# The odd layer's input projection: halves of rotated blocks taken one block later, and all its stores moved to the load queue

## The chip, the cores and the metric

The kernel runs on one core of one Trainium2 chip. The metric is the device time of one execution in microseconds (us). TensorE is called PE, VectorE DVE, ScalarE ACT, GpSimd POOL and SyncE SP. SP does nothing but issue DMAs. Line numbers (L1675) are those of the kernel before; in the changed kernel the same statements stand 2 to 14 lines further down.

## The reference, cut to what matters

A two-layer network on 256 context tokens and 2048 latent tokens of width 1024. Layer 0 (Fourier mixing and latent attention) is left as it is. Layer 1, the odd one, is grouped-query attention in a window of 128 tokens; this is what it projects:

```
q, k, v, g = split_cols(h_lat @ w_in, ODD_SPLITS)      # 1024, 256, 256, 1024 columns
q = apply_rope(q.reshape(b, n, 4, 4, 64), *rope)       # x1*cos - x2*sin, x2*cos + x1*sin
k = apply_rope(k.reshape(b, n, 4, 64), *rope)
ck, cv = split_cols(h_ctx @ w_in[:, 1024:1536], (256, 256))      # context: k and v, not rotated
y_l = (windowed_gqa(q, k, v, ck, cv, sink_hg) * silu(g)) @ w_out
```

## The kernel before, in words

**Items.** The tokens form nine chunks of 256 (chunk 0 is the context). The odd layer's input projection, at about 1820 to 2340 us of the span, walks over 15 steps, n = 0 to 14. A step is a group of chunks (1, 2, 3; then 4, 5, 6, 0; then 7, 8) with one block of 512 columns of the weights: the two halves of q, k with v, the two halves of the gate. In the first two groups the order is q, q, k/v, gate, gate (n = 0 to 4 and 5 to 9); in the third it is gate, gate, q, q, k/v (n = 10 to 14). A step consists of items (chunk i, half j), six for a q step of three chunks; an item of q, k or v is 48 matmuls of 128x256 into one of six PSUM banks (`ppm`). Every factor is held as two rounded halves, high and low, hence three products for one (`mm3`, L186 to L188).

**After an item.** `finish_t` rotates a q or k block: DVE multiplies by the two tables (L1675, L1676; the reading of PSUM ends here), POOL adds and subtracts (L1677, L1678), ACT rounds to the high half `rh` (L1679) and POOL subtracts for the low half `rl` (L1680). `rh` and `rl` have two buffers each. `store_t` writes the halves to DRAM (`q1h`, `q1l`, `kTh`, `kTl`) in four DMAs of 128 KB, issued by ACT (L1665). They are put in the list `pend`, and `flush` issues them behind the arithmetic of the next item. v goes through L1772, L1779, L1780 to `vd` (L1782), the gate through L1785 and L1789 to `g1d` (L1790), with ACT issuing too.

**Loads, all from SP.** While a step runs, the weights of the next (four loads of 512 KB) and later chunks of the input (`h1d`, two loads of 512 KB) come in and are split into halves by ACT (L180) with DVE or POOL (L183). The rope tables (`in_c_rope1c`, `in_c_rope1s`, 128 KB) have two buffers per kind; a step asks for its first two chunks' at its start and for the third's one chunk later. In step 1 eight blocks of weights of 128 KB (`in_o_w_in_t` 128x256, `bnd_load`) pass through two buffers: DVE takes absolute values (L1635) and PE multiplies (L1636), for a bound on v.

**The next stage** begins inside steps 13 and 14. `load_q6` loads the stored q of a query block of 128 tokens and one of four key heads in three DMAs (`sbr<-q1h`, `sbr<-q1l`). PE forms scores for the maxima (L1525, L1538) and DVE reduces them (L1529); then come the scores themselves (L1813 to L1815), ACT's exponentials (L1820) and the products with v (L1831 to L1833).

**What sets the order.** A scheduler puts the instructions of each engine in an order of its own. Only SP's DMAs are kept in the order of the program text: the class `sp` wraps each in `keep_in_program_order` (L150). An engine, SP too, issues in order and stands at an instruction that waits. Besides, each DMA waits until the one eight places before it, of SP's and ACT's together, has landed.

Of the kernel before, what the change touches and what calls it, by code (L numbers as in the profile page):

```python
# [10 lines left out]
F32 = mybir.dt.float32  # L11
F32R = mybir.dt.float32r
# [9 lines left out]
P = 128  # L22
# [119 lines left out]
def tile_hybrid(ctx: ExitStack, tc: tile.TileContext, A, out, dumps=None, stop=99):  # L142
    nc = tc.nc
    dumps = dumps or {}
    pe, act, dve, pool = nc.tensor, nc.scalar, nc.vector, nc.gpsimd
# [460 lines left out]
    for pi, chs in enumerate(PASSES):  # L606
# [12 lines left out]
        for oi, (ct, ci) in enumerate(order):  # L619
            if ct > seen:  # L620
# [4 lines left out]
                if ct >= 2 and nlater < len(later):  # L625
                    j = nlater
# [207 lines left out]
    for n_, (g, k) in enumerate(order):  # L834
# [14 lines left out]
        if k in (1, 3):  # L849
            q = ap_.tile([P, 512], F32, tag="qs", name=f"qs{g}_{k}")  # L850
            act.copy(q, res[k])
            if k == 1:
                pv = res[0][:, :, 0:256]
# [135 lines left out]
    def halves(dst, rows, src, n, name, e_lo=dve):  # L989

        eh = ep2.tile([P, 512], F32, tag="eh", name=f"{name}h")
        el = ep2.tile([P, 512], F32, tag="el", name=f"{name}l")
        act.copy(eh[:, 0:n].bitcast(F32R), src[:, 0:n])
        e_lo.tensor_sub(el[:, 0:n].bitcast(F32R), src[:, 0:n], eh[:, 0:n])
        flush2()

        def go():
            for d, r in zip(dst, (eh, el)):
                if isinstance(rows, int):
                    act.dma_start(d.rearrange("(h f d) t -> f h d t", f=2, d=16)[rows], r[:, 0:n])  # L1000
                else:
                    act.dma_start(d[rows, :], r[:, 0:n])

        pend2.append(go)
# [4 lines left out]
    for ci, (t0, n) in enumerate(CH):  # L1009
# [5 lines left out]
        for j in range(4):  # L1015
# [5 lines left out]
            e = ep2.tile([P, 512], F32, tag="eh", name=f"ek{ci}_{j}")  # L1021
# [581 lines left out]
    c5, b5, ep5 = sbuf(), sbuf(2), sbuf(3)  # L1603
# [51 lines left out]
    pend = []  # L1655

    def flush():
        while pend:
            pend.pop(0)()

    def store_t(rh, rl, i, rows):
        for r, kd, qd in ((rh, kTh, q1h), (rl, kTl, q1l)):
            dst = (kd[i] if rows is None else qd[i - 1][rows, :]).rearrange("(h f d) t -> f h d t", f=2, d=32)
            for f in range(2):
                act.dma_start(dst[f], r[:, f])  # L1665

    def finish_t(ps, n, i, rows):
        pv = ps.rearrange("p (f t) -> p f t", f=2)
        rh = ep5.tile([P, 2, 256], F32, tag="rh", name=f"rh5_{n}_{i}", bufs=2)
        rl = ep5.tile([P, 2, 256], F32, tag="rl", name=f"rl5_{n}_{i}", bufs=2)  # L1670
        if i:
            r = ep5.tile([P, 2, 256], F32, tag="ev", name=f"rt5_{n}_{i}")
            ct, st = (tabs[n, i, nm][:, None, :].to_broadcast([P, 2, 256]) for nm in ("ct", "st"))
            t = ep5.tile([P, 2, 256], F32, tag="tr", name=f"tt5_{n}_{i}", bufs=2)
            dve.tensor_mul(r, pv, ct)  # L1675
            dve.tensor_mul(t, pv[:, ::-1, :], st)  # L1676
            pool.tensor_sub(r[:, 0], r[:, 0], t[:, 0])  # L1677
            pool.tensor_add(r[:, 1], r[:, 1], t[:, 1])  # L1678
            act.copy(rh.bitcast(F32R), r)  # L1679
            pool.tensor_sub(rl.bitcast(F32R), r, rh)  # L1680
        else:
            act.copy(rh.bitcast(F32R), pv)
            dve.tensor_sub(rl.bitcast(F32R), pv, rh)
        flush()
        pend.append(lambda: store_t(rh, rl, i, rows))

    for n, (p, b) in enumerate(seq):
        bi = n % 5
        items = [(i, j) for i in P5[p] for j in range(2) if b == 2 or i]
        tb = [i for i in P5[p] if i] if b < 3 else []  # L1690
        for i in tb[0:1]:
            tab_load(n, i)
        fill = []
        if n == 0:
            fill += h5_steps(2) + fill5 + h5_steps(3)
        if n == 1:
            for q in (sm4, ppt):
                q.close()
            ppx = psum(2)
            fill += [bnd_open] + [lambda k=k: bnd_mm(k) for k in range(KT)] + [bnd_fin]  # L1700
        if p < 2:
            if bi == 3:
                fill += h5_steps(P5[p + 1][0])
        if p == 0 and bi == 4:
            pass
        if n == 10:
            x4p.close()
            x4p.tile([P, 2, 512], F32, tag="x", bufs=4)
            hs.close("s0", "s1")
        fill += w5_steps(n + 1)  # L1710
        late = []
        if p < 2 and bi == 4:
            late = P5[p + 1][1 : 3]
        if n == 5:
            fill = h5_steps(0) + fill
        e6n = []
        if n >= 11:
            e6n = e6.pop(0)
        tot = len(items) * KT
        done = 0  # L1720
        nf, ne = len(fill), len(e6n)
        w6n = []
        if n == 14:
            early6 = [f for x in range(TP["wa"] + 1) for f in (([lambda x=x: wload(*wl_[x])] if x < TP["wa"] else []) + ([lambda x=x: wsplit(*wl_[x - 1])] if x else []))]
            w6n, early6 = early6[:4], early6[4:]
        for x, (i, j) in enumerate(items):
            hh, hl = h5t[i]
            js = slice(j * P, (j + 1) * P)
            if b < 3 and not j and i in tb and tb.index(i) + 1 < len(tb):
                tab_load(n, tb[tb.index(i) + 1])  # L1730
            ps = ppm.tile([P, 512], F32, tag="mm", name=f"m5_{n}_{i}_{j}")
            for kk in range(KT):
                if b > 2:
                    wh, wl = w5t[n, kk]
                    mm3(ps, hh[:, kk, js], hl[:, kk, js], wh, wl, kk == 0, kk == KT - 1)
                else:
                    f, k0 = divmod(kk, 4)
                    o = ps[:, f * 256 : (f + 1) * 256]
                    fs = slice((2 * j + f) * P, (2 * j + f + 1) * P)
                    fj = slice(f * P, (f + 1) * P)  # L1740
                    for k in (2 * k0, 2 * k0 + 1):
                        wh, wl = w5t[n, k]
                        if b == 2 and j:
                            mm3(o, hh[:, k, fj], hl[:, k, fj], wh[:, 256:512], wl[:, 256:512], k == 0, k == KT - 1)
                        else:
                            mm3(o, wh[:, fs], wl[:, fs], hh[:, k, :], hl[:, k, :], k == 0, k == KT - 1)
                done += 1
                while fill and nf - len(fill) < nf * done / tot:
                    fill.pop(0)()
                while e6n and ne - len(e6n) < ne * done / tot:  # L1750
                    e6n.pop(0)()
                if w6n and done % 3 == 0:
                    w6n.pop(0)()
            if n == 14 and x == 1:
                while w6n:
                    w6n.pop(0)()
                hs.close("s2")
                w6n = early6
            if j == 1 and late:
                k_ = late.pop(0)  # L1760
                fs = h5_steps(k_)
                nf += len(fs)
                fill = fs + fill
            if b < 2:
                finish_t(ps, n, i, slice(b * 512 + j * 256, b * 512 + j * 256 + 256))
                continue
            if b == 2 and not j:
                finish_t(ps, n, i, None)
                continue
            e = ep5.tile([P, 512], F32, tag="ev", name=f"e5_{n}_{i}_{j}")  # L1770
            if b == 2:
                dve.tensor_mul(  # L1772
                    e.rearrange("p (f c) -> p f c", f=2), ps.rearrange("p (f c) -> p f c", f=2),
                    scl1[:, None, :].to_broadcast([P, 2, 256]),
                )
                vt = ep5.tile([P, 8, VW], F16, tag="vt", name=f"vt5_{n}_{i}", bufs=2)
                ev = e.rearrange("p (h d) -> p h d", d=64)
                pool.memset(vt[:, :, 64:VW], 1.0)
                act.copy(vt[:, :, 0:64], ev)  # L1779
                pool.tensor_sub(vt[:, :, 65:129], ev, vt[:, :, 0:64])  # L1780
                for f in range(2):
                    act.dma_start(vd[2 * i + f], vt[:, 4 * f : 4 * f + 4])  # L1782
            else:
                hf = b - 3
                act.activation(e, ps, AF.Silu)  # L1785
                ev = e.rearrange("p (k h d) -> p k h d", k=2, d=64)
                uv = uns1[:, hf * 128 : hf * 128 + 128].rearrange("p (k d) -> p k d", d=64)[:, :, None, :]
                for kk in range(2):
                    pool.tensor_mul(ev[:, kk], ev[:, kk], uv[:, kk].to_broadcast([P, 4, 64]))  # L1789
                act.dma_start(g1d[2 * i + j - 2][:, hf * 512 : (hf + 1) * 512], e)  # L1790
        flush()
        for f in fill + e6n + w6n:
            f()
        if n == 13:
            wgt.close(*[f"{t}{n % 2}{k}" for t in "hl" for k in range(KT)])
# [349 lines left out]
```

## Time and profile before

| | before |
|---|---|
| median of 3 runs | 3030.02 us (3030.01 to 3030.97) |
| profiled execution | 3034.24 us, span 3032.2 us |
| mean granted clock of PE | 0.983 |
| busy, share of the span | PE 94%, POOL 54%, DVE 48%, ACT 47% |

The span is what the trace covers, and all starting times are counted from its beginning. The granted clock is the share of PE's full speed that the chip allows; 1.00 is 2.4 GHz, 0.50 is 1.2 GHz. A busy time counts neither semaphore waits nor the issue of DMAs.

### The profile page before, as it was taken

To read this page: it belongs to the slowest core of one execution; us is meant where nothing else is said; L and a number is where in the kernel's file an instruction comes from. 1 tells how busy PE (TensorE), PEld (TensorE's weight loads), DVE (VectorE), ACT (ScalarE), POOL (GpSimd) and SP (SyncE) were. 2 spreads that over 40 slices of the span, in tenths; PEclk is the share of its full clock that TensorE was granted. 3 is DMA by queue.
4 is the path that set the end of the run, shared out by engine and by line. 5 is a ranking of instruction groups with operands and counts; after the bars stand their busy time and mean duration, and the time that the engine had idled before them with its cause. 6 is when DMAs were issued, how large, how long until landed. Compare 5 with 4: busy or idle time off the path is not lost. (4 is left out here: it accounts for less than half of the span.)

```text
span 3032.2 us, 54284 instructions
## 1 busy us (share of the span) xinstructions
PE 2861.0 (94%) x21388; PEld 2299.7 (76%) x21388; DVE 1462.6 (48%) x2884; ACT 1427.4 (47%) x2131; POOL 1632.0 (54%) x1221
## 2 busy tenths in 40 slices
PE   7999999999999999999999998999997899999998
PEld 4787777877777777777777888989786666677666
DVE  3323315453656665666542234323234666676664
ACT  4333213223577777777773332232222645554554
POOL 2202204035588888888784434353443766766665
PEclk9999999999999999999999998999998999999999
DMA  6453335466310111011016545544464333223321
GB/s 240 153 177 134 130 122 173 142 213 223 104 44 26 44 40 44 26 44 40 26 35 232 188 153 177 187 141 162 152 189 156 105 105 98 84 77 93 102 83 45
DMA packets 299399, 357.13 MB, mean 118 GB/s; under 512 B 40884, under 2 KB 210172, under 8 KB 299144
## 3 DMA queue, kind: packets, MB, share of 16 engines
q1 hardware_dynamic: 231320, 258.73, 27.0%
q10 hardware_dynamic: 67824, 94.93, 8.9%
q8 instruction: 168, 2.75, 0.4%
q14 instruction: 87, 0.71, 0.1%
HBM read 245.82 MB, written 107.76 MB: 117 GB/s over the span
## 5 line engine op out<-in xcount | busy, mean ns | idle before, releaser
L186 PE MATMUL psb<-sbr 128*128 128x512 f32 (+3 forms) x2054 | 744.3, 363 | 14.4 <-ACT sbf L1022 5.7
L188 PE MATMUL psb<-sbr 128*128 128x512 f32 (+3 forms) x2054 | 722.9, 352 | 4.8 <-DVE sbr L183 4.8
L187 PE MATMUL psb<-sbr 128*128 128x512 f32 (+3 forms) x2054 | 723.8, 352 | 2.2 <-POOL sbr L183 2.2
L1188 POOL TENSOR_TENSOR sbf<-sbf 128x1024 f16<-128x1024 f32 (+1 forms) x296 | 624.2, 2112 | 140.8 <-ACT sbf L1187 76.9
L155 PE MATMUL psb<-sbr 100*128 100x512 f32 (+1 forms) x2408 | 624.2, 399 | 21.0 <-DVE sbr L955 14.4
L155 PEld LDWEIGHTS psb<-sbr 100*128 100x128 f32 (+1 forms) x2408 | 425.0, 190 | 112.8 <-issue 17.3
L942 DVE TENSOR_REDUCE sbf<-psb 128x1 f32<-128x512 f32 (+1 forms) x584 | 400.7, 690 | 218.1 <-PE psb L155 203.5
L186 PEld LDWEIGHTS psb<-sbr 128*128 128x128 f32 (+1 forms) x2054 | 390.7, 190 | 81.0 <-issue 12.3
L188 PEld LDWEIGHTS psb<-sbr 128*128 128x128 f32 (+1 forms) x2054 | 390.2, 190 | 63.9 <-DVE sbr L183 6.8
L187 PEld LDWEIGHTS psb<-sbr 128*128 128x128 f32 (+1 forms) x2054 | 390.8, 190 | 53.2 <-POOL sbr L183 3.9
L1821 POOL TENSOR_TENSOR sbf<-sbf 128x512 f16<-128x512 f32 x282 | 338.0, 1213 | 116.0 <-issue 60.1
L1186 ACT ACTIVATE sbf<-psb 128x1024 f32<-128x1024 f32 (+1 forms) x296 | 299.6, 1012 | 200.4 <-PE psb L155 180.5
L183 DVE TENSOR_TENSOR sbr<-sbf,sbr 128x512 fp32r<-128x512 f32 (+3 forms) x212 | 209.1, 1014 | 382.2 <-ACT sbr L180 381.1
L180 ACT CAST sbr<-sbf 128x512 fp32r<-128x512 f32 (+4 forms) x286 | 198.2, 731 | 394.5 <-PE psb L187 149.5
L183 POOL TENSOR_TENSOR sbr<-sbf,sbr 128x512 fp32r<-128x512 f32 (+4 forms) x113 | 166.1, 1482 | 367.9 <-ACT sbr L180 226.3
L1819 ACT ACTIVATE sbf<-psb 128x512 f32<-128x512 f32 x312 | 188.4, 604 | 282.1 <-PE psb L1815 249.8
L1187 ACT ACTIVATE sbf<-psb 128x1024 f16<-128x1024 f32 (+1 forms) x296 | 297.8, 1006 | 0.0
L155 PEld LDWEIGHTS <-sbf 128*128 128x128 f16 x4672 | 213.5, 97 | 72.9 <-issue 65.9
L155 PE MATMUL psb<-sbf 128*128 128x129 f16 (+1 forms) x4672 | 256.8, 207 | 5.2 <-DVE sbf L1214 2.9
L1529 DVE CUSTOM_DVE_ANT_0 sbf<-psb,sbf 128x384 bf16<-128x384 f32 (+1 forms) x256 | 137.8, 538 | 119.4 <-PE psb L1525 108.1
L1820 ACT ACTIVATE sbf<-psb 128x512 f16<-128x512 f32 x312 | 188.2, 603 | 5.5 <-DMA vd<-sbf 5.5
L1831 PEld LDWEIGHTS <-sbf 128*128 128x128 f16 x1248 | 115.5, 97 | 68.3 <-issue 61.8
(259 smaller groups left out, 4303.9 us busy)
## 6 DMA issues: line engine op xcount, KB each, us to landing
sbf<-in_o_w_in_t SPq DMA_DIRECT2D x60, 512.0 KB
sbf<-in_w_in_t SPq DMA_DIRECT2D x54, 512.0 KB
sbf<-in_x SPq DMA_DIRECT2D x32, 512.0 KB
sbf<-in_w_mod SPq DMA_DIRECT2D x32, 512.0 KB
sbr<-q1h SPq DMA_DIRECT2D x128, 128.0 KB
h1d<-sbf ACTq DMA_DIRECT2D x9, 1024.0 KB
sbf<-h1d SPq DMA_DIRECT2D x18, 512.0 KB
x1d<-sbf ACTq DMA_DIRECT2D x16, 512.0 KB
```

The costliest lines, as they stand in the source:

```text
L155: tc.keep_in_program_order(nc.tensor.matmul(*args, **kw))
L180: act.copy(hi, src)
L183: e_lo.tensor_sub(lo, src, hi)
L186: pe.matmul(ps, sh, mh, start=start, stop=False)
L187: pe.matmul(ps, sh, ml, start=False, stop=False)
L188: pe.matmul(ps, sl, mh, start=False, stop=stop)
L942: dve.reduce_max(st["mx"][:, js[0] : js[-1] + 1, c], ps[:, 0 : len(js) * kn].rearrange("p (j k) -> p j k", k=kn), axis=AX.X)
L1186: act.activation(pf[:, :, 0:n], ps[:, :, 0:n], AF.Exp, scale=MLA_SCALE)
L1187: act.activation(ph[:, :, 0:n], ps[:, :, 0:n], AF.Exp, scale=MLA_SCALE)
L1188: pool.tensor_sub(pl[:, :, 0:n], pf[:, :, 0:n], ph[:, :, 0:n])
L1819: act.activation(pf, ps, AF.Exp, scale=GQA_SCALE)
L1821: (dve if (TP["b0"].get("sub", TP["sub"]) if b == 0 else TP["sub"])[kv][n] else pool).tensor_sub(pl, pf, ph)
```

## The change

`flush` no longer empties the list but runs as many entries as stood in it on entry. A rotated block now enters `pend` with its halving; run at the next item, the halving puts the store in the list, and the item after that issues it. So halves are taken one item later and stored one more. At the end of a step `while pend: flush()` empties the list. The unrotated k of the context is halved at once. The stores of q, k, v and the gate are issued by `sp.dma_start`, so on SP, in the order of the program text among the loads, where ACT issued them; those of v and the gate too wait one item.

```diff
--- before.py
+++ after.py
@@ -1655,19 +1655,21 @@
     pend = []
 
     def flush():
-        while pend:
+        for _ in range(len(pend)):
             pend.pop(0)()
 
     def store_t(rh, rl, i, rows):
         for r, kd, qd in ((rh, kTh, q1h), (rl, kTl, q1l)):
             dst = (kd[i] if rows is None else qd[i - 1][rows, :]).rearrange("(h f d) t -> f h d t", f=2, d=32)
             for f in range(2):
-                act.dma_start(dst[f], r[:, f])
+                sp.dma_start(dst[f], r[:, f])
 
     def finish_t(ps, n, i, rows):
         pv = ps.rearrange("p (f t) -> p f t", f=2)
-        rh = ep5.tile([P, 2, 256], F32, tag="rh", name=f"rh5_{n}_{i}", bufs=2)
-        rl = ep5.tile([P, 2, 256], F32, tag="rl", name=f"rl5_{n}_{i}", bufs=2)
+
+        def halves():
+            return [ep5.tile([P, 2, 256], F32, tag=t, name=f"{t}5_{n}_{i}", bufs=2) for t in ("rh", "rl")]
+
         if i:
             r = ep5.tile([P, 2, 256], F32, tag="ev", name=f"rt5_{n}_{i}")
             ct, st = (tabs[n, i, nm][:, None, :].to_broadcast([P, 2, 256]) for nm in ("ct", "st"))
@@ -1676,13 +1678,22 @@
             dve.tensor_mul(t, pv[:, ::-1, :], st)
             pool.tensor_sub(r[:, 0], r[:, 0], t[:, 0])
             pool.tensor_add(r[:, 1], r[:, 1], t[:, 1])
+        else:
+            flush()
+            rh, rl = halves()
+            act.copy(rh.bitcast(F32R), pv)
+            dve.tensor_sub(rl.bitcast(F32R), pv, rh)
+            pend.append(lambda: store_t(rh, rl, i, rows))
+            return
+        flush()
+
+        def halve():
+            rh, rl = halves()
             act.copy(rh.bitcast(F32R), r)
             pool.tensor_sub(rl.bitcast(F32R), r, rh)
-        else:
-            act.copy(rh.bitcast(F32R), pv)
-            dve.tensor_sub(rl.bitcast(F32R), pv, rh)
-        flush()
-        pend.append(lambda: store_t(rh, rl, i, rows))
+            pend.append(lambda: store_t(rh, rl, i, rows))
+
+        pend.append(halve)
 
     for n, (p, b) in enumerate(seq):
         bi = n % 5
@@ -1778,8 +1789,9 @@
                 pool.memset(vt[:, :, 64:VW], 1.0)
                 act.copy(vt[:, :, 0:64], ev)
                 pool.tensor_sub(vt[:, :, 65:129], ev, vt[:, :, 0:64])
+                flush()
                 for f in range(2):
-                    act.dma_start(vd[2 * i + f], vt[:, 4 * f : 4 * f + 4])
+                    pend.append(lambda d=vd[2 * i + f], v=vt[:, 4 * f : 4 * f + 4]: sp.dma_start(d, v))
             else:
                 hf = b - 3
                 act.activation(e, ps, AF.Silu)
@@ -1787,8 +1799,10 @@
                 uv = uns1[:, hf * 128 : hf * 128 + 128].rearrange("p (k d) -> p k d", d=64)[:, :, None, :]
                 for kk in range(2):
                     pool.tensor_mul(ev[:, kk], ev[:, kk], uv[:, kk].to_broadcast([P, 4, 64]))
-                act.dma_start(g1d[2 * i + j - 2][:, hf * 512 : (hf + 1) * 512], e)
-        flush()
+                flush()
+                pend.append(lambda d=g1d[2 * i + j - 2][:, hf * 512 : (hf + 1) * 512], e=e: sp.dma_start(d, e))
+        while pend:
+            flush()
         for f in fill + e6n + w6n:
             f()
         if n == 13:
```

What this does to the order shows at three places. The first is SP at the end of step 0. Before, with the loads of the next step's weights, the tables of step 1 and the eight blocks of the bound in a row (`h1d3` is the input of chunk 3, `sbf_62` on-chip memory):

```order
L150 DMA sbf_62<-h1d3_5182 128x4x256 x2
L150 DMA sbf_62<-in_o_w_in_t 128x2x512 x4
L150 DMA sbf_62<-in_c_rope1c 128x256
L150 DMA sbf_62<-in_c_rope1s 128x256
L150 DMA sbf_62<-in_c_rope1c 128x256
L150 DMA sbf_62<-in_c_rope1s 128x256
L150 DMA sbf_62<-in_o_w_in_t 128x256 x8
```

Now, from the stores of the third item on (`q1h1` is chunk 2's high half; each row is two DMAs):

```order
L150 DMA sbf_62<-in_o_w_in_t 128x2x512 x2
L150 DMA q1h1_15987<-sbf_62 4x32x256 x2
L150 DMA q1l1_15995<-sbf_62 4x32x256 x2
...
L150 DMA q1h2_15988<-sbf_62 4x32x256 x2
L150 DMA q1l2_15996<-sbf_62 4x32x256 x2
L150 DMA sbf_62<-in_c_rope1c 128x256
L150 DMA sbf_62<-in_c_rope1s 128x256
L150 DMA sbf_62<-in_c_rope1c 128x256
L150 DMA sbf_62<-in_c_rope1s 128x256
L150 DMA sbf_62<-in_o_w_in_t 128x256 x8
```

All stores of step 0 stand ahead of step 1's tables and of the eight blocks. The same holds wherever q or k steps follow one another. The first store of step 1 in turn stands behind the eight blocks. On PE the first product with such a block (L1636) was the 41st matmul of step 1 and is now the 80th; from it to the seventh there were 72 matmuls and are now 66.

The second place is ACT in step 0, at the splits of chunk 3's input (L180). Before:

```order
L1665 DMA q1l_15994<-sbf 4x32x256 x2
L1679 CAST sbf<-sbf 128x512
L180 CAST sbr<-sbf 128x512 x3
L1665 DMA q1h_15987<-sbf 4x32x256 x2
L1665 DMA q1l_15995<-sbf 4x32x256 x2
L180 CAST sbr<-sbf 128x512 x3
```

Now (L1692 is the high half, L1679 before):

```order
L1366 ACTIVATE sbf<-psb,sbf 128x256 x3
L1374 DMA h1d_5179<-sbf 128x8x256
L1692 CAST sbf<-sbf 128x512
L180 CAST sbr<-sbf 128x512 x4
L1692 CAST sbf<-sbf 128x512
L180 CAST sbr<-sbf 128x512 x4
```

The rounding ahead of the splits is now that of the item before, and no issue stands between.

The third place is SP around step 14. Before, the q loads of the next stage (`sbr_58`) stand among loads alone:

```order
L150 DMA sbf_62<-in_c_rope1s 128x256
L150 DMA sbr_58<-q1h0_15986 64x4x128
L150 DMA sbr_58<-q1l0_15994 64x4x128
L150 DMA sbr_58<-q1h0_15986 64x4x128 x2
...
L150 DMA sbf_62<-in_o_w_out 128x512 x6
L150 DMA sbf_62<-g1d0_16002 128x1024
L150 DMA sbr_58<-q1h0_15986 64x4x128
L150 DMA sbr_58<-q1l0_15994 64x4x128
```

Now they follow the last stores of step 13, and those for query block 1 the last of step 14:

```order
L150 DMA q1h7_15993<-sbf_62 4x32x256 x2
L150 DMA q1l7_16001<-sbf_62 4x32x256 x2
L150 DMA sbf_62<-in_c_rope1c 128x256
...
L150 DMA sbr_58<-q1h0_15986 64x4x128
L150 DMA sbr_58<-q1l0_15994 64x4x128
...
L150 DMA vd16_16052<-sbf_62 128x520
L150 DMA vd17_16053<-sbf_62 128x520
L150 DMA sbf_62<-in_o_w_out 128x512
L150 DMA sbf_62<-g1d0_16002 128x1024
L150 DMA sbr_58<-q1h0_15986 64x4x128
```

The q loads of head 0 (step 13) likewise follow step 12's last stores. On PE the scores for block 1's maxima, which stood between block 0's first scores, now follow five of these; the first maxima of step 14 come 39 matmuls later.

## Rows read from the trace of the kernel before

**Rows 1.** Stretches of core 0: busy us (and count) of each engine, granted clock, DMA share, GB/s.
```profile
1910.00:2010.00 100.00, 100.00 (x583) 87.77 (x582) 24.13 (x35) 29.80 (x53) 42.29 (x47) 1.00 0.53 180
...
2280.00:2320.00 40.00, 29.09 (x204) 28.54 (x203) 17.04 (x37) 7.46 (x13) 14.25 (x15) 0.83 0.47 151
2320.00:2360.00 40.00, 29.02 (x204) 23.77 (x204) 17.61 (x49) 15.86 (x29) 20.22 (x19) 0.74 0.50 152
```

**Rows 2.** Waits of PE, 1820 to 2360 us: total us, times, longest.
```profile
PE psb L1636 <- DVE sby L1635: 2.7, 2, 1.4
...
PE psb L186 <- ACT sbf L1785: 2.8, 1, 2.8
...
PE psb L1813 <- ACT sbf L1820: 1.7, 1, 1.7
```

**Rows 3.** Timeline of PE, 1850 to 1858: start, duration, instruction, [idle before <-releaser].
```profile
1852.80 0.38 PE L186 MATMUL psb<-sbr 128*128 128x256 f32 x1 [1.68 <-ACT sbr L180]
1854.85 0.58 PE L187 MATMUL psb<-sbr 128*128 128x256 f32 x1 [1.67 <-POOL sbr L183]
```

**Rows 4.** Timeline of ACT and its DMA issues (ACTq), 1849 to 1880.
```profile
1851.61 0.62 ACT L1679 CAST sbf<-sbf 128x512 fp32r<-128x512 f32 x1 [3.49 <-POOL sbf L1678]
...
1876.11 1.83 ACTq L1665 DMA_DIRECT2D q1l<-sbf  x2
```

**Rows 5.** Stretches at half clock: PE busy, granted clock, DMA share, GB/s.
```profile
1853.86:1860.69 6.83, 5.79 (x25) 0.50 0.35 125
1881.17:1888.00 6.83, 5.92 (x27) 0.50 0.41 139
```

**Rows 6.** Timeline of SP's DMA issues from 1866 on.
```profile
1869.60 17.86 SPq L150 DMA_DIRECT2D sbf<-in_o_w_in_t  x8
```

**Rows 7.** Timeline of DVE, 1825 to 1890.
```profile
1867.86 0.69 DVE L1675 TENSOR_TENSOR sbf<-psb,sbf 128x512 f32<-128x512 f32 x1 [1.11 <-PE psb L188]
...
1874.69 0.42 DVE L1635 SCALAR_TENSOR_TENSOR sby<-sbf 128x256 fp32r<-128x256 f32 x1 [5.55 <-DMA sbf<-in_o_w_in_t]
...
1889.70 0.41 DVE L1635 SCALAR_TENSOR_TENSOR sby<-sbf 128x256 fp32r<-128x256 f32 x1
```

**Rows 8.** Timeline of PE, 1871 to 1885.
```profile
1870.78 0.28 PE L186 MATMUL psb<-sbr 128*128 128x256 f32 x1
1870.89 0.28 PE L187 MATMUL psb<-sbr 128*128 128x256 f32 x1
...
1875.22 0.36 PE L1636 MATMUL psb<-sby 128*128 128x256 f32 x1 [2.74 <-issue]
```

**Rows 9.** Issues that write `q1l`, 2018 to 2112: min/median/max ns, first and last start.
```profile
L1665 ACTq DMA_DIRECT2D q1l<-sbf x24: 532/558/1811, 2029.6 to 2108.5; - x24
```

**Rows 10.** Timeline of PE at the start of n = 7.
```profile
2083.83 0.39 PE L186 MATMUL psb<-sby,sbr 128*128 128x256 f32 x1 [0.49 <-ACT sbr L180]
```

**Rows 11.** Timeline of PE, 2280 to 2356: the waits at the scores' maxima.
```profile
2282.10 0.36 PE L1525 MATMUL psb<-sbr 128*128 128x256 f32 x1 [0.25 <-DMA q1h<-sbf]
...
2293.54 0.58 PE L1525 MATMUL psb<-sbr 128*128 128x256 f32 x1 [7.43 <-DVE sbf L1529]
...
2311.92 0.55 PE L1525 MATMUL psb<-sbr 128*128 128x256 f32 x1 [3.22 <-DMA sbr<-q1l]
...
2338.63 0.69 PE L1525 MATMUL psb<-sbr 128*128 128x384 f32 x1 [2.30 <-DMA sbr<-q1l]
...
2349.61 0.98 PE L1525 MATMUL psb<-sbr 128*128 128x384 f32 x2 [6.25 <-DMA sbr<-q1l]
```

**Rows 12.** The chain that ended last at 2356: start, us, what.
```profile
2279.72 10.86 DMA q1l<-sbf
...
2311.85 6.65 DMA q1l<-sbf
...
2347.21 4.45 DMA vd<-sbf
```

**Rows 13.** Timeline of SP's DMA issues, 2270 to 2320.
```profile
2274.38 0.58 SPq L150 DMA_DIRECT2D sbr<-q1h  x1
```

## The prediction

> **What bounds the kernel now.** I read the stretches first. In the middle of the changed part PE is busy for all of 100.00 us at full clock; at its end, where the next stage begins, it is busy for 29.09 and 29.02 of 40 us at clocks of 0.83 and 0.74 [rows 1]. So in the steps themselves PE is the bound, every other engine has slack, and only two things move the end: us in which PE idles, and the half clock that follows an idle spell. The waits of PE and its timeline then say where it idles. There are five places: 1.68 + 1.67 us in step 0 at splits of chunk 3 [rows 3]; 2.74 and 2.7 us at the bound's products in step 1 [rows 2, 8]; 2.8 us, the longest of a few, behind a PSUM bank that a gate item holds [rows 2]; 0.25 + 7.43 us in step 13 and 3.22 us in step 14, before scores for maxima [rows 11]; and 2.30 + 6.25 + 1.7 us before block 0's first exponentials can be used [rows 2, 11]. The stretches at 1.2 GHz of 6.83 us each [rows 5] cost about half their length.
>
> **What the change removes: issues on ACT.** An issue instruction of ACT waits for the data and for an older DMA, and ACT's arithmetic behind it waits with it. In step 0 the splits of chunk 3 stood behind the rounding of 1851.61, which had waited 3.49 us for POOL [rows 4]. Now the rounding ahead of the splits is an item old and there is no issue. I count the 3.35 us of idleness as gone, and half of the 6.83 us at half clock from 1853.86 [rows 5] for a part: 1.9 of 3.4. Gain 5.3 us; bounds 0 (the splits wait for the chunk's load instead) and 6.8. What hides a later store is the slack of the other engines: the q stored in step 0 is read from 2274.38 on [rows 13], and rounding one item later costs nothing while the two buffers suffice. That cover ends at the ends of steps.
>
> **What it adds: loads behind stores.** SP issues in order, so a table or weight load now waits until the stores before it have data, a place among eight DMAs, and have gone out. In step 0 the last rotation begins on DVE at 1867.86 [rows 7] and its last two stores are issued from 1876.11 on, each issue taking part of 1.83 us [rows 4], so until 1877.9. With step 0 shorter by 3.6 us, 1874.3. Then four tables follow and the first block of the bound, at some 0.6 us each 2.4 us later. In the trace the first of the eight issues at 1869.60 [rows 6] and DVE can start at 1874.69 [rows 7], 5.1 us. That puts DVE's first absolute value at 1881.8 and the first product at 1882.2. Matmuls follow one another every 0.12 us [rows 8], so step 1, begun at 1867.8 before and 1864.2 now, reaches its 80th matmul at 1873.6: **PE waits 8.6 us** where it waited 2.74.
>
> The rest of that loop runs on two buffers: first to seventh start on DVE take 15.0 us [rows 7], and PE has 66 matmuls in between, 7.8 us, so it idles 7.2 us more. Before, the 72 matmuls were 8.6 us of the same 15.0, and the trace shows the 6.4 us as 2.7 us of idleness [rows 2] and some 3.4 us of half clock [rows 5]. Together 15.8 against 9.1: loss 6.7, taken as 7. Bounds: +1 (stores of the last item go out as soon as the halves exist, 1872, and the blocks land faster) and +14 (they land like a loaded store, 10.86 us [rows 12], in place of 5.1).
>
> The eight loads take 17.9 us [rows 6], and step 1's first store now stands behind them, at about 1895, 15 us later than an item's end allows. Stores are then paced: in steps 5 and 6, 24 issues to `q1l`, two an item, span 78.9 us [rows 9], so 6.7 us an item. Step 1's stores end near 1935, step 2's tables and step 3's weights come after them, and the last of these weights behind step 2's first k and v stores, at about 1948; with 5.1 us to land and 2 us of splits, 1955. Step 3 begins at 1864.2 + 68.4 (two steps of six items of 5.7 us) + 15.8 = 1948.4 and wants that weight three quarters through its first item, 1952.7. Loss 3 us, bounds 0 and 12.
>
> In steps 5 to 7 the same lag meets the six PSUM banks. Step 7 begins at 2083.83 [rows 10] and can run six items, 34 us, until its first block must have left its bank, 2118. Its tables stand behind step 6's last stores, which ended at 2108.5 [rows 9]; with the tables' issue and 5.1 us they land at 2116. So a wait of 0 to 5 us at the edge, and again a weight (step 8) behind stores, replaces the 2.8 us [rows 2]. Loss 1.5, bounds -5 and +12.
>
> **The start of the next stage.** In step 13 the q loads were issued from 2274.38 on [rows 13] and were in time: PE waited only 0.25 us at 2282.10 [rows 11]. Now they follow the last store of step 12, issued at 2279.72 [rows 12], four tables and a weight, which is some 5 us with their own issue, and land at 2290: 8 us of idleness. The 7.43 us at 2293.54 [rows 11] go: that wait ran through DVE to ACT, which stood behind a store issue that lasted until the store of 2279.72 had landed. These two cancel to within a us. In step 14 the loads follow the store of 2311.85 [rows 12] and land near 2321, while PE, 39 matmuls later in its order, arrives at 2313: 8 us against 3.22, loss 4.8. Block 1's loads follow the last v store (2347.21 for chunk 8 in the trace [rows 12]) and land near 2357, but PE has five scores and their products to do first; I count 7 us of waits against 10.3, gain 3.3. Sum +2, bounds -12 and +12.
>
> **Sum.** -5.3 + 7 + 3 + 1.5 + 2 = +8.2 us. On the profiled execution (3034.24 us, of which 3032.2 are the span) that is 3042.4; the profiled execution lies 4.2 us above the median of the runs, so against 3030.02 I predict **3038 us**.
>
> **A rule against the change.** With two issuing engines, loads in the trace landed in 5.1 us beside stores that took up to 10.86 us [rows 7, 12]. The Trainium skill, page "DMA: Bandwidth & Descriptors", section "Queues, rings and completion order", says that each DMA engine takes turns, packet by packet, between the queue rows that have work, and that SP and ACT own one row each. By it a load that now shares the row with stores would stand behind them and land more like a store; the sum would gain about 5.8 us at each place where PE waits for a load. No row of this kernel shows one row alone, so this stands as a rival.
>
> **The rivals.**
> - *Loads land like stores.* At the four waits above (the bound's first block, steps 13 and 14, block 1) 10.86 replaces 5.1: +23 on top of 8.2, about 3061 us. For it: 24 pairs of stores ran at 6.7 us an item where PE needs 5.7 [rows 9]. Against it: at the ends of steps few stores are left in flight.
> - *Faster: freeing ACT decides.* The 7.43, 2.30, 6.25 and 1.7 us of [rows 2, 11] go, because the q loads, of old data, are issued before PE gets there; step 14's wait grows by 5. Then -5.3 + 7 + 3 - 17.7 + 5 = -8, and 3022 us. It decides from the point at which the first load of head 0 is issued before about 2277. Against it: step 12's last store was issued at 2279.72, for reasons (the pace of stores) that the change leaves.
> - *Nothing moves.* What ACT loses in waiting, SP waits, and the stalls change place: 3030 us. The page named above says in "Rules for kernel authors" that spreading DMAs over SP and ACT gives no bandwidth and saves only the sequencer's issue time. By that rule the time would not move either way, as ACT is off the path in the steps. The trace agrees for the middle steps (PE 100.00 of 100.00 us [rows 1]); no run shows the rest.
>
> **Chances.** The forecast's case (3034 to 3050) 0.40; loads like stores or further boundary waits (3050 to 3068) 0.17; no change 0.18; faster 0.25. A measurement of this kernel tells about 0.2% from no change, 6 us, so slower above 3036, faster below 3024; a part of the forecast's case falls within that. Slower 0.54, same 0.20, faster 0.26. The range leaves out the far ends: 3018 to 3061; that of the forecast's case alone is 3034 to 3050.
>
> **What would show it.** Right: PE idle for 6 us or more before the first L1636 product (behind L1635), the eight blocks issued from about 1877; no wait of PE at splits of chunk 3; the first L1525 of step 13 waiting on a q load and the 7.43 us behind DVE gone. Wrong: q loads of head 0 issued before 2277, or table loads issued within 2 us of the last rotation; then stores go out faster than I took, and the time falls. A PE wait of over 10 us inside steps 2 to 8 would be the rival with slow loads or a full set of PSUM banks.

## The result

The changed kernel takes 3067.91 us (median of 4 runs, 3060.54 to 3070.9), the kernel before beside it 3030.49 us. The ratio is 1.012 with a 95% interval of 1.0106 to 1.0134: slower by 1.2%. The profiled execution has a span of 3067.1 us where the one before had 3032.2, so 34.9 us have to be found.

The middle of the changed part, which PE filled before [rows 1], now reads, in the same columns:

```profile
1910.00:2010.00 100.00, 91.99 (x545) 79.60 (x544) 26.94 (x38) 26.05 (x47) 36.59 (x41) 0.97 0.45 142
```

PE idles for 8 of 100 us there. The waits of PE in the changed kernel, 1820 to 2400 us (total, times, longest), and below them what the first of these groups was before, 1820 to 2360 us:

```profile
PE psb L186 <- ACT sbr L180: 14.7, 4, 5.7
PE psb L1525 <- DMA q1h<-sbf: 13.6, 1, 13.6
PE psb L1636 <- issue: 13.5, 1, 13.5
PE psb L1827 <- ACT sbf L1834: 7.3, 1, 7.3
PE psb L1525 <- DMA sbr<-q1l: 6.4, 2, 5.9
```

```profile
PE psb L186 <- ACT sbr L180: 2.2, 2, 1.7
```

Against [rows 2, 11] the 7.43 us behind DVE in step 13 are no longer there, the wait at L1636 has grown from 2.74 to 13.5 us, one on a q load of 13.6 us has come, and splits of loads (L180) have grown from 2.2 to 14.7 us. To place them I counted PE's matmuls L186 to L188. Each item of a q, k or v step has 48 of the 256-column form and each gate item 24 of the 512-column form, so the start of every step can be read off. The third column is by how much the step ran longer than before (end of 14: its last matmul):

```
step      before     after   longer by
0         1819.9    1820.9    -5.1
1         1867.6    1863.5    +8.4
2         1911.9    1916.2    +1.0
3         1945.9    1951.2    +1.1
4         1979.3    1985.7   +11.0
5         2012.7    2030.1    +2.1
6         2046.6    2066.0    -1.3
7         2081.8    2099.9    +6.4
8         2129.0    2153.5    -4.8
9         2167.2    2186.9    +4.6
10 to 12  2202.3    2226.6     0.0
13        2269.6    2293.8    +6.0
14        2303.2    2333.4    +3.9
its end   2334.9    2369.0    (the rest of the span: +0.7)
```

With the 1.0 us that step 0 starts later this makes 34.9. Each column is read from one execution, so small differences say little: in the traces of the runs below step 0 starts between 4.0 us earlier and 1.1 us later than before, and in run 12, which moves two loads and nothing else, the lengths of steps 0, 6, 7 and 8 differ by 1.8 to 3.2 us. The reading rests on the losses of about 4 us and more.

**Step 1** went as forecast. SP's issues in the changed kernel, 1862 to 1900:

```profile
1872.82 2.54 SPq L150 DMA_DIRECT2D q1h<-sbf  x2
1875.46 2.86 SPq L150 DMA_DIRECT2D q1l<-sbf  x2
1878.42 1.18 SPq L150 DMA_DIRECT2D sbf<-in_c_rope1c  x1
...
1881.12 14.35 SPq L150 DMA_DIRECT2D sbf<-in_o_w_in_t  x8
...
1897.98 1.09 SPq L150 DMA_DIRECT2D q1h<-sbf  x2
```

and DVE's and PE's timeline beside it:

```profile
1866.56 0.68 DVE L1677 TENSOR_TENSOR sbf<-psb,sbf 128x512 f32<-128x512 f32 x1
...
1885.23 0.69 DVE L1677 TENSOR_TENSOR sbf<-psb,sbf 128x512 f32<-128x512 f32 x1 [17.40 <-DMA sbf<-in_c_rope1c]
...
1886.57 1.29 DVE L1635 SCALAR_TENSOR_TENSOR sby<-sbf 128x256 fp32r<-128x256 f32 x2
```

```profile
1887.10 0.55 PE L1636 MATMUL psb<-sby 128*128 128x256 f32 x1 [13.50 <-issue]
```

The last rotation of step 0 starts at 1866.56, the issue of its last store ends only at 1878.3 (each pair takes some 2.5 us to get out), then come the tables and at 1881.12 the eight blocks that had started at 1869.60 [rows 6]. DVE sits idle for 17.40 us and PE for 13.50.

**Step 4** I had not looked at. SP, ACT and POOL in the changed kernel, 1964 to 2000:

```profile
1969.31 1.04 SPq L150 DMA_DIRECT2D vd<-sbf  x2
1970.40 2.74 SPq L150 DMA_DIRECT2D sbf<-h1d  x2
1978.86 0.33 SPq L150 DMA_DIRECT2D g1d<-sbf  x1
1979.23 0.98 SPq L150 DMA_DIRECT2D sbf<-in_o_w_in_t  x2
1985.44 0.34 SPq L150 DMA_DIRECT2D g1d<-sbf  x1
1985.82 0.43 SPq L150 DMA_DIRECT2D sbf<-in_o_w_in_t  x1
1992.68 0.34 SPq L150 DMA_DIRECT2D g1d<-sbf  x1
1993.06 0.43 SPq L150 DMA_DIRECT2D sbf<-in_o_w_in_t  x1
```

```profile
1968.49 0.60 ACT L1797 ACTIVATE sbf<-psb 128x512 f32<-128x512 f32 x1
1978.21 1.14 ACT L180 CAST sby<-sbf 128x512 fp32r<-128x512 f32 x2 [9.12 <-DMA sbf<-h1d]
...
1980.70 0.59 ACT L1797 ACTIVATE sbf<-psb 128x512 f32<-128x512 f32 x1
...
1989.58 0.62 ACT L180 CAST sbr<-sbf 128x512 fp32r<-128x512 f32 x1 [3.22 <-DMA sbf<-in_o_w_in_t]
1990.10 0.59 ACT L1797 ACTIVATE sbf<-psb 128x512 f32<-128x512 f32 x1
...
1997.41 1.14 ACT L180 CAST sbr<-sbf 128x512 fp32r<-128x512 f32 x2 [5.71 <-DMA sbf<-in_o_w_in_t]
```

```profile
1990.77 3.25 POOL L1801 TENSOR_TENSOR sbf<-sbf 128x256 f32<-128x256 f32 x4 [5.35 <-ACT sbf L1797]
```

PE's waits there, and of SP's own waits from 1820 to 2400 the two longest in total:

```profile
1990.25 0.50 PE L186 MATMUL psb<-sbr 128*128 128x512 f32 x1 [1.42 <-ACT sbr L180]
...
1998.08 0.79 PE L186 MATMUL psb<-sbr 128*128 128x512 f32 x1 [5.23 <-ACT sbr L180]
```

```profile
SPq L150 <- ACT sbf L1797: 62.6, 16, 6.8
SPq L150 <- POOL sbf L1801: 56.1, 30, 5.6
```

SP, ACT and POOL wait for one another in a ring. It begins where the load of chunk 4's input (`h1d`) stands behind step 2's v stores: ACT, in order, stands 9.12 us at the split of that load, and behind the split is the gate's activation (L1797). The gate's store waits for this activation and for POOL's multiplication after it (L1801), and step 4's weights stand behind the gate's stores. One lap can be read off: the weight load of 1985.82 releases ACT's split at 1989.58, the activation follows at 1990.10, POOL's multiplication at 1990.77, then the store at 1992.68 and the last weight load at 1993.06, 7.2 us after the one before.

How far SP runs ahead shows what was lost. Counted off in the same way as the matmuls, the last of step 4's four weight loads was issued 34.7 us ahead of the step in the kernel before and 7.4 us into the step in the changed one; for step 9 it was 39.6 us ahead and is 4.4 us into it. With loads alone SP ran that far ahead of PE; with stores among them it stands until the data of each store exist.

**Step 13.** SP in the changed kernel, first where steps 11 and 12 meet, then ahead of the q loads:

```profile
2270.07 3.93 SPq L150 DMA_DIRECT2D g1d<-sbf  x2
...
2286.30 1.26 SPq L150 DMA_DIRECT2D q1h<-sbf  x2
...
2304.74 2.54 SPq L150 DMA_DIRECT2D q1l<-sbf  x2
2307.38 1.10 SPq L150 DMA_DIRECT2D sbf<-in_c_rope1c  x1
...
2311.31 0.63 SPq L150 DMA_DIRECT2D sbr<-q1h  x1
```

The q load waits for step 12's stores as forecast. But these began only at 2286.30, because loads for the next stage stand between them and the last gate stores of step 11, which went out at 2270.07 to 2274.

### The profile page after: what moved, and what is told of

Read it like the earlier page. It is cut to its first block, busy times and chain, and to the rows that moved or that the text cites. A ratio compares the mean times of both kernels' runs of the same rounds, so it can differ in the third digit from the quotient of the medians.

```text
span 3067.1 us, 54254 instructions
## 1 busy us (share of the span) xinstructions
PE 2869.1 (94%) x21371; PEld 2303.4 (75%) x21388; DVE 1472.9 (48%) x2884; ACT 1428.3 (47%) x2131; POOL 1637.0 (53%) x1221
## 5 line engine op out<-in xcount | busy, mean ns | idle before, releaser
L186 PE MATMUL psb<-sbr 128*128 128x512 f32 (+3 forms) x2054 | 743.8, 362 | 13.4 <-ACT sbr L180 6.7
L188 PE MATMUL psb<-sbr 128*128 128x512 f32 (+3 forms) x2054 | 723.3, 352 | 4.3 <-DVE sbr L183 4.3
L186 PEld LDWEIGHTS psb<-sbr 128*128 128x128 f32 (+1 forms) x2054 | 389.8, 190 | 79.8 <-issue 12.3
L188 PEld LDWEIGHTS psb<-sbr 128*128 128x128 f32 (+1 forms) x2054 | 389.4, 190 | 63.5 <-DVE sbr L183 6.4
L183 DVE TENSOR_TENSOR sbr<-sbf,sbr 128x512 fp32r<-128x512 f32 (+3 forms) x212 | 220.4, 1062 | 374.1 <-ACT sbr L180 367.8
L180 ACT CAST sbr<-sbf 128x512 fp32r<-128x512 f32 (+4 forms) x286 | 199.7, 731 | 410.7 <-PE psb L187 146.2
L1529 DVE CUSTOM_DVE_ANT_0 sbf<-psb,sbf 128x384 bf16<-128x384 f32 (+1 forms) x256 | 137.8, 538 | 109.7 <-PE psb L1525 98.5
L1834 ACT ACTIVATE sbf<-psb 128x512 f16<-128x512 f32 x312 | 187.9, 603 | 3.6 <-DMA vd<-sbf 3.6
```

The source lines that it names most:

```text
L180: act.copy(hi, src)
L183: e_lo.tensor_sub(lo, src, hi)
L186: pe.matmul(ps, sh, mh, start=start, stop=False)
L188: pe.matmul(ps, sl, mh, start=False, stop=stop)
```

## The experiments

All kernels compute the whole reference. Ratios are to the kernel before, run beside them on the same chip; its median lay between 3030 and 3037 us from one set of runs to another, so ratios are compared, and the profiled executions step by step.

**1. Only the delay.** The changed kernel with every `sp.dma_start` of a store turned back:

```diff
-                sp.dma_start(dst[f], r[:, f])
+                act.dma_start(dst[f], r[:, f])
```
(and the same for `vd` and `g1d`)

> The changed kernel, with its stores issued by ACT again; halves and stores stay one item later. Theory (the loss is loads that stand behind stores on SP): the five places of the loss vanish and the shorter step 0 stays, about 3025 us, 3015 to 3034. Rival (taking halves and stores later costs, by buffers held longer): above 3045 us, with the waits of steps 4, 7 and 13 still there.

Measured: 1.0001 (0.9989 to 1.0013), median 3030.92 us. Its waits of PE:

```profile
PE psb L1525 <- DMA sbr<-q1l: 14.3, 5, 6.1
PE psb L1636 <- issue: 4.5, 1, 4.5
...
PE psb L186 <- ACT sbf L1797: 2.7, 1, 2.7
```

The splits of loads by ACT are gone from the list, and steps 3 to 6 and 9 to 12 last as long as before to within 1.3 us. So the loss comes with the issue on SP. Not all went as expected: step 0 is not shorter in this run (0.0), and step 1 is still 3.1 us longer, with 4.5 us at L1636 where it was 2.7 before.

**2. Only the issue on SP.** The kernel before, all its stores through `sp.dma_start`.

> The kernel before, with all stores of the projection issued by SP; halves and stores at the same place in the program as before. Theory (loads behind stores): as slow as the changed kernel or slower, 3055 to 3085 us, with a wait of over 10 us before the first product of the bound (L1636). Rival (the later halves cost): within 8 us of 3030.

Measured: 1.0208 (1.0192 to 1.0224), median 3093.16 us, more than expected. Its waits of PE begin so:

```profile
PE psb L186 <- ACT sbr L180: 26.3, 10, 5.0
PE psb L1636 <- issue: 11.4, 1, 11.4
PE psb L1525 <- DMA q1h<-sbf: 11.0, 1, 11.0
```

With halves taken at once SP waits at nearly every item for the data (17 waits for ACT's rounding L1679 alone, 50.9 us), and ten waits for splits take 26.3 us where the changed kernel had 14.7 in four. Taking halves and stores an item later is therefore neutral with ACT issuing (run 1) and worth about 25 us with SP issuing: without it this change would cost 2.1% and not 1.2%.

**3. The gate's stores back on ACT.**

```diff
-                pend.append(lambda d=g1d[...], e=e: sp.dma_start(d, e))
+                pend.append(lambda d=g1d[...], e=e: act.dma_start(d, e))
```

> The changed kernel, with the gate's stores alone back on ACT. Theory (each boundary has its own loads behind its own stores): the 11.0 us that step 4 lost and the 4.5 of step 9 come back, the rest stays: 3048 to 3058 us. Rival (one shared row of DMA slows all loads alike): less than 5 us come back, over 3063.

Measured: 1.0034 (1.002 to 1.0048), median 3040.27 us: some 27 us come back, more than expected. Steps 4 and 9 are back to their old length (0.0 and +0.2), as expected, but step 13 too (-1.0). Its SP, where step 12's first store and the first q load go out:

```profile
2261.50 1.15 SPq L150 DMA_DIRECT2D q1h<-sbf  x2
...
2284.35 0.63 SPq L150 DMA_DIRECT2D sbr<-q1h  x1
```

Step 12's first store leaves 9.5 us after its step begins (2252.0), where it was 15.1 in the changed kernel (2271.2), and the wait at the first q load is 6.5 in place of 13.6 us. So step 13's loss was also the gate's, carried on by SP's order. The weights are ahead of their steps again, though by less than before: the last of step 4's goes out 9.2 us ahead of it, that of step 9's 7.1. Left are steps 1 (+8.1) and 7 (+6.2, with -4.8 in step 8) and 14 (+4.1).

**4. The list is not emptied at a step's end.** `while pend: flush()` only in step 14, so the last halves and stores of a step go into the next.

> The changed kernel, without emptying the list at the end of each step: the last halves and stores of a step are carried into the first items of the next, so that its tables, the first blocks of the bound and the q loads stand ahead of them on SP. Theory: the wait before the first product of the bound falls from 13.5 us to below 6, those of steps 13 and 14 (13.6 and 5.9) to below 6 together; step 4 keeps its loss: 3040 to 3055 us. Rival (the stores' pace, not their place before the loads): over 3062.

Measured: 1.0102 (1.0084 to 1.0121), median 3062.15 us, above the theory's 3055 and, by 0.15 us, in the rival's range. The waits at the three places shrink, if not as far as expected (7.2 us at L1636 and 4.3 at a later product, 4.0 and 3.7 at the q loads). But against the kernel before step 2 now runs 5.4, step 5 5.4 and step 9 7.0 us longer, where the changed kernel lost 1.0, 2.1 and 4.6, and 10.0 us of waiting for exponentials (L1834) have come after step 14. The waits follow the stores' place; carried on, the stores make other loads late.

**5. Two of the bound's blocks loaded in step 0.**

```diff
-        bnd_load(0)
-        bnd_load(1)
...
-            fill += h5_steps(2) + fill5 + h5_steps(3)
+            fill += h5_steps(2) + fill5 + h5_steps(3)[:2] + [lambda: bnd_load(0), lambda: bnd_load(1)] + h5_steps(3)[2:]
```
(the first two lines stood in `bnd_open`, which belongs to step 1)

> The changed kernel, with the first two of the bound's eight blocks of weights loaded in step 0, ahead of its stores; the other six stay in step 1, behind the last stores of step 0. Theory (the place on SP decides): the 13.5 us before the first product (L1636) go, but the third block still comes late, so a wait of 5 to 13 us appears before the third product; step 1 loses 2 to 7 us in place of 8.4, the total 3060 to 3067. Rival (the wait is set by DVE or by PE's new order, not by the loads): the first product waits as before and nothing moves.

Measured: 1.0111 (1.0096 to 1.0126), median 3068.49 us, just above the expected 3060 to 3067; step 1 loses 7.1 us. PE (L1634 is the product here):

```profile
1867.31 0.38 PE L186 MATMUL psb<-sbr 128*128 128x256 f32 x1 [3.50 <-ACT sbr L180]
...
1885.25 0.58 PE L1634 MATMUL psb<-sby 128*128 128x256 f32 x1 [8.62 <-DVE sby L1633]
```

and SP:

```profile
1876.50 1.19 SPq L150 DMA_DIRECT2D sbf<-in_c_rope1c  x1
...
1879.16 10.16 SPq L150 DMA_DIRECT2D sbf<-in_o_w_in_t  x5
```

The first product no longer waits, the third does, for 8.62 us: its block leaves behind the stores. The place of the load on SP sets the wait; nothing is won, since step 1's own weights became late too (the 3.50 us above, in its first item).

**6. Only q's and k's stores back on ACT,** the complement of run 3: the first line of run 1's edit alone.

> The changed kernel, with the stores of q and k back on ACT; those of v and the gate stay on SP. The complement of the run with the gate alone on ACT. Theory: the wait before the bound's first product falls to 3 to 5 us as in the kernel before, step 4 still loses about 11 us and step 9 about 4, step 13 a part: 3043 to 3058 us. Rival (only the sum of stores on SP counts): each half gives back in proportion to its DMAs, 108 of 150 here, under 3041 us and step 4 loses less than 5 us.

Measured: 1.0051 (1.0034 to 1.0068), median 3051.19 us, in the theory's range, but not place by place. (The trace of the changed kernel has 164 stores of q and k on SP out of 214, not 108 of 150.) The wait at L1636 is 7.6 us and not 3 to 5, step 4 loses only 2.4 us, as the rival had it, and step 5 loses 8.1 in its stead, step 9 loses 4.9 and step 13 4.5; and 10.3 us are lost after step 14, with PE's 11.2 us wait for block 0's exponentials. There ACT's timeline shows

```profile
2358.82 1.57 ACT L1834 ACTIVATE sbf<-psb 128x512 f16<-128x512 f32 x3 [3.02 <-DMA vd<-sbf]
```

so it waits for a v store that SP issued late. The changed kernel shows the same there, 3.59 us, and its 7.3 us at L1827. That the exponentials take over the room of v's tile is likely, but was not tried.

**7. The weights of steps 4 and 9 ahead of the gate's stores.**

```diff
-        fill += w5_steps(n + 1)
+        w5s = w5_steps(n + 1)
+        if n in (3, 8):
+            fill = [w5s.pop(x) for x in (0, 0, 2, 4)] + fill
+        fill += w5s
```

> The changed kernel, with the four weight loads for steps 4 and 9 moved to the start of steps 3 and 8, ahead of the gate's stores on SP; nothing else. Theory: the loss in step 3 to 4 that PE shows as waits for splits (1.4 and 5.2 us with half clock, 11.0 us in all) falls below 4 us, that of steps 8 and 9 below 3; 3050 to 3060 us. Rival (ACT's splits are late because ACT is behind with the gate, whatever SP does): step 4 still loses over 8 us.

Measured: 1.0061 (1.0043 to 1.008), median 3053.23 us, as expected. The four popped entries are the loads; the last of them now goes out 12.4 us ahead of step 4 and 10.2 ahead of step 9. Step 4 loses 0.0 us (11.0 before this edit) and step 9 is 1.7 shorter than in the kernel before: it was the place of the weights, and ACT was not otherwise behind. But step 5 now loses 8.6 us in place of 2.1, by the same kind of wait:

```profile
PE psb L186 <- ACT sbr L180: 4.1, 1, 4.1
```

**8. Gate on ACT, two blocks in step 0, the q load of head 0 in step 12.** Runs 3 and 5 together, and `load_q6(0, 0)` moved one step ahead.

> The changed kernel with the gate's stores on ACT, the first two blocks of the bound in step 0, and the q load of head 0 in step 12 in place of 13. Theory: from 3040 us, the 6.5 us wait of step 13 goes and a part of step 1's loss: 3025 to 3036. Rival: waits move on to the next load and the total stays at 3038 to 3042.

Measured: 1.0043 (1.0028 to 1.0058), median 3046.92 us: no better than run 3, as the rival said. In step 13 the wait for the q load gives way to 7.6 us behind DVE (L1529).

**9 to 11. Toward a faster version.** Run 9 is run 1 with run 5's early blocks. Run 10 is run 3 with the stores of a step's end on ACT as well:

```diff
+        q5[0] = act
         while pend:
             flush()
+        q5[0] = sp
```
(the stores of q, k and v are issued through `q5[0]`, which is `sp` elsewhere)

Run 11 is run 10 with the early blocks.

> All stores back on ACT, halves still one item later, and the first two blocks of the bound loaded in step 0. With no stores on SP the early load should now pay: the wait before the bound's first products (4.5 us with ACT issuing) falls below 2, and the total is 3 to 6 us below that run, 3024 to 3029. Rival (as with the stores on SP, the wait moves to the third product and to splits of weights): within 2 us of 3031.

> The changed kernel with the gate's stores on ACT and, of the q, k and v stores, those of a step's last two items (the ones issued when the list is emptied at the step's end) on ACT too; the others stay on SP. Theory: what was left at the ends of steps with the gate alone on ACT goes with it: the 13.5 us before the bound's first product fall to 3 to 8, the 6.2 us that step 7 lost and the 6.0 us wait of step 14 to below 3 each; 3022 to 3033 us. Rival (the stores in the middle of a step on SP delay loads as much): over 3036.

> The run before, and the first two blocks of the bound in step 0. Theory: the wait before the bound's products falls by 2 to 6 us more; 3018 to 3030 us. Rival: waits move to the third product, no change.

Measured: 0.9987 (0.9976 to 0.9999), 0.9994 (0.9981 to 1.0007) and 0.9993 (0.9982 to 1.0004). In run 10 the losses of steps 7 (-0.6) and 14 (+0.4) are gone, as expected, with the stores in the middle of steps still on SP, though the q load of step 14 is still waited for, for 4.5 us. The wait at L1636 is not gone: 12.8 us where 3 to 8 were expected. SP, and its longest wait from 1862 to 1874, show why:

```profile
1863.04 1.19 SPq L150 DMA_DIRECT2D sbf<-in_c_rope1c  x1
...
1871.31 0.33 SPq L150 DMA_DIRECT2D sbf<-in_c_rope1s  x1
1872.04 14.12 SPq L150 DMA_DIRECT2D sbf<-in_o_w_in_t  x8
```

```profile
SPq L150 <- DMA q1l<-sbf: 6.1, 2, 3.7
```

The first two tables leave early, but the blocks come 9 us after the first of them. In between SP stands until its own last two `q1l` stores, issued from 1860.08 on, have landed, and then until the first table has: by the trace's completion events that was at 1868.53, 1871.24 and 1871.97, and each time the next issue follows within 0.1 us. That is the order in which the eighth DMA before has to land; that this rule is the reason was not tried by itself. In this kernel's order PE also arrives at the product 5.5 us into the step and not 10.1.

In run 9 step 1 is 1.6 us shorter than before, and the ratio lies 0.0014, or 4 us, under that of run 1, as expected, though the two intervals overlap. The wait before the first product is gone; 4.0 us stand before a later one. Run 11 went as its rival said: no change against run 10, and the longest wait of 6.6 us now stands before a later product.

**12. The early blocks in the kernel before,** nothing else.

> The kernel before, with nothing but the first two blocks of the bound loaded in step 0 (halves at once, stores on ACT). Theory (the later halves do nothing by themselves): as with halves one item later and the same early load, a ratio of 0.997 to 1.000 to the kernel before. Rival (the small gain of that run came from the later halves): 1.000 to 1.003.

Measured: 0.9999 (0.9987 to 1.001). That is where the ranges of theory and rival meet, and its interval and that of run 9 overlap, so whether the later halves add anything there stays open. Run 9 alone has an interval below 1, by 0.0001 at its upper end; with four versions tried, that is not shown to be a gain.

## Why the prediction was wrong

The direction held, and so did the mechanism, loads that stand behind stores on SP, at the places that the prediction looked at. It left out a place where the same mechanism cost most: 3068 us against a range that ended at 3061. By its own steps:

```
step of the prediction                 forecast   measured
splits of chunk 3 (step 0)               -5.3       -5.1
the bound's blocks (step 1)              +7         +8.4
a weight in step 3 (steps 2, 3)          +3         +2.1
steps 5 to 8                             +1.5       +2.4
the next stage (steps 13, 14, after)     +2        +10.6
steps 4 and 9                             0        +15.6
start of step 0                           -         +1.0
sum                                      +8.2      +34.9
```

- **Splits of chunk 3.** The size came out right by luck. PE still waits 1.6 + 0.3 us there, and 3.41 us at half clock follow in place of 6.83, so the place itself gave some 3.2 us. Much of the rest is a stretch of 3.41 us at half clock from 1833.38 on in the trace before, which the changed kernel's trace does not have (clock 1.00 from 1820.9 to 1853.0). And step 0 is not shorter in run 1 but 4.0 us shorter in run 6, which both issue step 0's stores from ACT and take halves late, and 2.6 us shorter in run 12, which takes them at once; so what the delay gives there is not settled.
- **The bound's blocks.** Right in kind, a little small: the last stores left SP at 1878.3, not 1874.3, since pairs went out 2.5 us apart. The first wait was 13.5 us where I had 8.6, and the two-buffer loop behind it cost 1.0 us of idleness where I had 7.2; that the two errors nearly cancel is luck. (The working moves step 1 forward by 3.6 us where the sum counts 5.3. Both times in the wait move with it, so the 8.6 stays.)
- **Steps 5 to 8.** The sum is near, the parts are not: a weight that was late by 5.7 us in step 7 in place of full PSUM banks, and 4.8 us won in step 8. Step 7 of the kernel before began at 2081.8; the 2083.83 of [rows 10] is a wait 2.0 us into it.
- **Steps 4 and 9: the step that failed.** The prediction followed the loads behind stores of q and k at the ends of steps and counted the gate steps among those where "PE is the bound, every other engine has slack". It listed no load behind a gate store and put these steps at 0. There the store depends on ACT and POOL, ACT on a load, and the next load on the store, and ACT, for all its slack, stood waiting for loads: steps 4 and 9 cost 15.6 us, and run 7 takes this out of them by moving eight loads, run 3 by moving the gate's stores. Of the prediction's signs the wait at L1636, the late blocks and the q load of step 13 came, and the wait at the splits of chunk 3 did not go. A wait of over 10 us inside steps 2 to 8, its sign of more, did not come: the loss there lies in shorter waits, 5.7 us at most, with half clock behind them.
- **The next stage.** The forecast took step 12's last store from the trace before, 2279.72, some 10 us after step 13 began at 2269.6. It left at 2307.3, 13.5 after the step began at 2293.8, as gate stores and other loads were in front (run 3: at 2280.9, 6.2 after the step began, and half of the wait). The gain of 3.3 at block 1 did not come either: 7.3 us of waiting for exponentials stand there.

Of the rivals, the total is nearest to that of loads landing like stores, but not for its reason. The first block, issued at 1881.12, was used by DVE at 1886.57, so 5.45 us later where it was 5.1 before [rows 6, 7]; the table that released DVE just before took 6.8 (1878.42 to 1885.23). Over the whole projection loads landed much as before: by the completion events of the two traces the 512 KB weight loads took 5.9 us in the median (6.1 before), the tables 5.3 (4.8 before) and the 512 KB loads of the input 5.7 (6.3 before), where the rival took 10.86. And the row was now nearly alone: from 1820 to 2340 us the queue that holds SP's DMAs took 47.6% of the 16 DMA engines' time and ACT's 1.2%, against 31.2% and 19.0% before. The Trainium skill, page "DMA: Bandwidth & Descriptors", section "Queues, rings and completion order", says that each DMA engine takes turns between the queue rows that have work; the longer landings that the prediction took from it for one row these medians do not show. What was late is the issue. "Nothing moves" fell too: the rule that the prediction took from the same page of the Trainium skill, "Rules for kernel authors", is about bandwidth, and the loss here is in the order of issue.

## What to carry to other kernels

A queue that issues in order ties whatever is put into it to all that stands behind: before stores are moved among loads, list for every load which store now precedes it and which engine that store waits for, in every stage and not only at the ends. Read from the trace before how far ahead of its use each load goes out; that lead (34.7 us for step 4's weights) is what stores in the same queue can take away. Look for rings (load, engine, store, next load); one lap took 7.2 us here. Moving loads ahead made others late in runs 5, 7 and 8; moving the gate's stores, which depend on ACT and POOL, to the other queue gave back nearly three quarters of the loss.

## What was not expected of the hardware

Single executions of the kernel before spread from 3024.8 to 3044.9 us over the later sets of runs, after 3030.01 to 3030.97 in the first three, so differences of 0.2% needed ten runs and more a side. Where loads came late the DMA engines were not full: between 1910 and 2010 us they were busy for a share of 0.45 and moved 142 GB/s, against 0.53 and 180 GB/s before [rows 1]. Issuing a store took longer in a row of stores: 0.56 us is the median of an issue to `q1l` on ACT in steps 5 and 6 before [rows 9], while on SP the twelve stores from 1861 to 1878 left one after another at 1.4 us each, with hardly a wait between them.
